# A fourth state block in another PSUM bank, and a chunk attention whose broadcast opens inside its second block

## The chip, the core and the metric

The kernel runs on one core of one Trainium2 chip. The metric is the device time of one execution in microseconds (us). Three runs of the kernel before gave 981.59, 984.75 and 985.48 us (median 984.75). Everything that is read from a profile belongs to one profiled execution, which took 984.45 us, 982.5 of them inside the recorded span.

TensorE (PE) multiplies matrices into PSUM banks, PEld is its weight load, VectorE (DVE), ScalarE (ACT) and GpSimd (POOL) work elementwise, and SyncE (SP) issues nearly all DMA transfers. The granted clock of TensorE is given as a share of full speed: 1.00 is 2.4 GHz, 0.50 is 1.2 GHz.

## The reference

A two-layer encoder trunk over 512 frames of width 1024, in float32, with cross-attention into 256 memory tokens behind each layer. What bears on the change:

```python
# layer 0
z = rms_norm(x, g) @ w_in          # w_in: 1024 x 2560 = 20 blocks of 128 columns
u_a, gate_a, val_b, glu_b, gate_b = split(z)     # 512 columns (4 blocks) each
y_a = s5_mixer(u_a, ...) * silu(gate_a)          # diagonal complex state space, associative scan
y_b = conv_module(val_b, glu_b, ...) * silu(gate_b)   # v = val * sigmoid(glu), depthwise conv of 31 taps
x = x + concat(y_a, y_b) @ w_out
x = x + mem_cross_attention(...)
# layer 1
q, k, v, g = split(rms_norm(x, g) @ w_in, 4)     # 16 heads of 64
s = q k^T / 8 + bias                             # chunks of 64, each sees 8 chunks back
x = x + (softmax(s) v * silu(g)) @ w_out
```

rms_norm divides each frame by the root of its mean square and multiplies with a gain per channel.

## The kernel before

**Layout.** Channels lie on the 128 partitions and the 512 frames along the free dimension. The row factor of rms_norm (one number per frame) is left out of the normalised input h and multiplied in behind each product: the factor of a frame is computed from the sum of squares on a column, put on a diagonal matrix (`dg`), and broadcast over the partitions by TensorE as `ps_acc<-dg,ones`; `rb_tile` (L276) copies the result to the tile `rb`. An eviction then multiplies a block of products by `rb`.

**Three products.** A float32 product is made of two parts each: `split` (L173) casts a value to the short format on ScalarE (`whi<-raw`) and subtracts the cast from the value (`wlo<-raw,whi`), on GpSimd unless an engine is named. A block of 128 output channels is 24 matmuls of 128x512: for each of 8 slices of the input, weight-high times h-high and weight-high times h-low (16 with `whi`), then 8 with `wlo`. In the rows, 16 products stand as `ps_proj<-h,whi x16`. `weights` (L178) issues the load of a weight block (512 KB) on SyncE's queue into one of 3 `raw` tiles; there are 2 `whi` and 3 `wlo` tiles.

**PSUM.** The eight banks are shared out by name: three "proj", two "att", two "tr", one "acc" (`PS`, L127). A tile of a name takes the bank whose last user is through. `proj` (L201) makes a layer-0 block in a "proj" bank. The "tr" banks hold transposes.

**Layer 0.** After the first state blocks, the first convolution blocks, the third state block and the broadcast, the order of the instructions is no longer the program's: `T.ordered` is set to False, jobs are emitted by the string PLAN (L706), and the scheduler of the framework sets the order on each engine from its own estimate, with priority for what stands under `tc.high_priority()`:

```python
PLAN = "u0 u1 z0 c0 u2 u3 z1 c1 g0 k0 t0 g1 k0 k0 a0 z2 b0 c2 k0 v1 ..."
```

u is a state block (`state_input`, L865: products, scaling by rb, two DMAs that reorder it), z and c are a convolution's gate and value block (`conv_gate`, `conv_input`), g an output gate, k four taps of the first convolution on VectorE (`conv_sums`, tile ps_proj_562), t the tables of the state space, a, b and o the parts of a scan, v the taps of the other convolutions on TensorE, whose matrices `cw` are loaded by SyncE. u3 is the fourth state block. In it, before, the tile in the order's numbering is ps_proj_424. In `conv_input`, the value v (tile x, `x<-ps_proj,ev`) multiplies a value block with its gate and frees the value block's bank.

**Chunk attention.** Here the order is the program's. `first()` (inside `chunk_attention`, L1169) opens it: the first query block (`od_qkg[0]`), `st.done()`, which computes the row factor from the sum of squares with small instructions of VectorE (128x4) and ends in the diagonals, the first key block (`od_qkg[1]`), the broadcast, and the scaling of both (`qk_finish`). `qk_finish` scales into z, and splits it into high and low halves on ScalarE and GpSimd or VectorE (tiles qk). Two blocks wait in "proj" banks until `rb` is there. Then a filler puts a further block (the first gate block, 24 products) between the score products (`ps_att<-qk,qk`), with `fill.run(START)`, START = 3.0 us by the program's own count, ahead of the first score. Blocks of this kind come from `unit` (L1033), a generator that emits one product per step.

Of the kernel before, what the change touches and what calls it, by code (L numbers as in the profile page):

```python
# [18 lines left out]
SEQ = 512  # L19
# [25 lines left out]
def kernel(  # L45
# [23 lines left out]
    V, A, G = nc.vector, nc.scalar, nc.gpsimd  # L69
# [59 lines left out]
    def psum(tag):  # L129
        return pp.tile([P, 512], F32, tag=tag, name=nm("ps_" + tag), bufs=PS[tag])  # L130
# [19 lines left out]
    def pinned(ins):  # L150
        tc.keep_in_program_order(ins)
# [26 lines left out]
    def weights(src, kt=8, n=P, eng=None, tag="whi"):  # L178
        raw = tl("raw", (P, kt, n))
        nc.sync.dma_start(raw, src)  # L180
        hi = rl(tag, (P, kt, n))
        lo = rl("wlo", (P, kt, n))
        with tc.high_priority():
            split(raw, hi, lo, eng)
        return hi, lo
# [12 lines left out]
        for i, (a, b) in enumerate(prods):  # L198
            T.matmul(ps, a, b, start=(i == 0), stop=(i == len(prods) - 1))

    def proj(w, act, n=SEQ, cuts=()):  # L201
        ps = psum("proj")
        wh, wl = w
        mm3(ps[:, :n], [((wh[:, k, :], wl[:, k, :]), act[k]) for k in range(wh.shape[1])], cuts)
        return ps
# [70 lines left out]
    def rb_tile(rs):  # L276
        ps = bcast(rs, SEQ)
        t = tl("rb")
        A.copy(t, ps)
        return t  # L280
# [440 lines left out]
    ps = psum("acc")  # L721
# [141 lines left out]
    uP, U, ys, gates = [None] * 4, [None] * 4, [], [None] * 8  # L863

    def state_input(i):  # L865
        ps = proj(weights(w_in_d[3], eng=V), h0) if i == 3 else third if i == 2 else first_ps[i]
        t = tl("uu", (P, 4, NJ))
        with tc.high_priority():
            tt(t.rearrange("p s j -> p j s"), ps.rearrange("p (j s) -> p j s", s=4),
               rb0.rearrange("p (j s) -> p j s", s=4), ALU.mult)  # L870
        ud = dr.tile([4, 32, 4, NJ], F32, name=nm("ud"))
        nc.sync.dma_start(ud.rearrange("q c s j -> (q c) s j"), t)
        u = tl("uu", (P, 4, NJ))
        for s in range(4):
            nc.sync.dma_start(u[s * 32:(s + 1) * 32], ud[:, :, s, :].rearrange("q c j -> c q j"))
        uP[i] = t
        U[i] = u
# [152 lines left out]
            prods += [(ah, bh), (ah, bl)]  # L1030
        return prods + [(al, bh) for (ah, al), (bh, bl) in terms]

    def unit(wsrc, act, finish, last=None, tag="whi", cols=slice(0, SEQ)):  # L1033
        wh, wl = weights(wsrc, tag=tag)
        n = cols.stop - cols.start
        ps = psum("proj")[:, :n]
        prods = products([((wh[:, k, :], wl[:, k, :]), act[k]) for k in range(last or len(act))])
        for i, (a, b) in enumerate(prods):
            pinned(T.matmul(ps, a, b[:, cols], start=(i == 0), stop=(last is None and i == len(prods) - 1)))
            yield 0.2135 * n / SEQ  # L1040
        finish(ps, wh, wl)

# [126 lines left out]
    def chunk_attention(h, st, w_d):  # L1169
# [26 lines left out]
        def first():  # L1196
            late = []

            def keep(ps, wh, wl):
                late.append(ps)  # L1200
            for t in unit(od_qkg_d[0], h, keep):
                yield t
            norm["rs"] = st.done()

            klo.extend([(rl("sq"), rl("sq")), (rl("kl"), rl("sa"))])
            for pair in klo:
                for e, t in enumerate(pair):
                    G.memset(f(t[64 * (1 - e):64 * (2 - e)]), 0.0)
            for t in unit(od_qkg_d[1], h, keep):
                yield t  # L1210
            norm["rb"] = rb_tile(norm["rs"])
            for e in range(2):
                qk_finish(0, e)(late[e], None, None)

# [3 lines left out]
        def g_unit(hp):  # L1218
            def finish(ps, wh, wl):
                gs[hp] = silu_gate(ps, norm["rb"])  # L1220

            return ("g", hp), unit(od_qkg_d[3 * hp + 2], h, finish)

        def v_unit(gr):
            def gen():
# [345 lines left out]
```

## Time and profile before

| | before |
|---|---|
| median of 3 runs | 984.75 us (981.59 to 985.48) |
| profiled execution | 984.45 us |
| span in it | 982.5 us |
| mean granted clock | 0.987 |
| TensorE busy | 948.6 us, 97% of the span |
| VectorE busy | 582.6 us, 59% |
| ScalarE busy | 467.8 us, 48% |
| GpSimd busy | 441.2 us, 45% |

The busy time of TensorE counts its instructions from start to end, at whichever clock they ran; a matmul that runs at the lower clock is longer busy. In rows of the trace, "out<-in" names the tiles without their numbers, and a bracket at the end gives the idle time of the engine before the instruction and who ended it.

### The profile page before, as it was taken

The numbers are of one execution on the slowest core, as the hardware profiler recorded it, in microseconds if no ns is written. First come the engines' busy times: TensorE is split into PE (matmuls) and PEld (weight loads), VectorE is DVE, ScalarE is ACT, GpSimd is POOL, SyncE is SP. The second block draws the span as 40 slices with busy tenths as digits, with TensorE's granted clock in tenths as the row PEclk, the third lists the DMA queues.
The fourth block names the chain that finished last, engine by engine and source line by source line (L and its number), as shares of the span: only waits on it lengthen the run. The fifth ranks groups of instructions, "written<-read, shape, count | busy, mean of one in ns | idle before, by whom it ended". The sixth has DMA issues, their size and how long they took to land.

```text
span 982.5 us, 14196 instructions
## 1 busy us (share of the span) xinstructions
PE 948.6 (97%) x5256; PEld 809.9 (82%) x5256; DVE 582.6 (59%) x1404; ACT 467.8 (48%) x844; POOL 441.2 (45%) x245
## 2 busy tenths in 40 slices
PE   8998999989999999999999999999999999999996
PEld 7787989758888888888798887878788998888895
DVE  7999746883344343552568777688667313433476
ACT  7243446474443434434366555656545443343352
POOL 1013343059676344457454434444327983434241
PEclk9998999999999999999999999999999999999998
DMA  8253555356422222122222222222114552122153
GB/s 294 100 163 111 166 178 179 101 166 230 161 97 90 82 70 81 65 96 89 84 77 86 82 74 70 75 79 72 65 45 139 171 179 101 65 86 85 44 171 109
DMA packets 50245, 110.05 MB, mean 112 GB/s; under 512 B 11137, under 2 KB 22529, under 8 KB 50177
## 3 DMA queue, kind: packets, MB, share of 16 engines
q1 hardware_dynamic: 49888, 109.07, 33.2%
q8 instruction: 41, 0.67, 0.3%
q14 instruction: 28, 0.22, 0.1%
q10 hardware_dynamic: 288, 0.08, 0.0%
HBM read 103.37 MB, written 5.77 MB: 111 GB/s over the span
## 4 chain that ended last, share of the span: by engine, by line
PE 34%; DVE 10%; ACT 3%; issue 2%; POOL 1%; DMA 1%; POOLq 0%; DVEq 0%; ACTq 0%
PE ps_proj L82 27%; PE ps_att L82 2%; PE ps_tr L85 2%; DVE pe L159 2%; DVE ps_att L1301 1%; PE ps_acc L82 1%; DVE o L154 1%; ACT whi L174 1%; DVE h L163 1%; PE ps_tr L82 1%; ACT pe L1288 1%; POOL wlo L154 1%; DVE z L154 1%; DVE s L1300 1%; DVE qk L154 1%
## 5 line engine op out<-in xcount | busy, mean ns | idle before, releaser
L154 POOL TENSOR_TENSOR wlo<-raw,whi 128x1024 fp32r<-128x1024 f32 x130 | 317.1, 2443 | 412.3 <-ACT whi L174 378.5
L82 PE MATMUL ps_proj<-h,whi 128*128 128x512 f32 x1184 | 301.7, 400 | 5.6 <-DVE x L154 3.3
L82 PEld LDWEIGHTS ps_proj<-h,whi 128*128 128x128 f32 x1184 | 220.6, 191 | 51.5 <-issue 8.0
L174 ACT CAST whi<-raw 128x1024 fp32r<-128x1024 f32 x148 | 155.2, 1049 | 192.2 <-PE ps_proj L82 87.0
L82 PE MATMUL ps_proj<-h,wlo 128*128 128x512 f32 x592 | 151.5, 393 | 0.0
L82 PE MATMUL ps_proj<-og,whi 128*128 128x512 f32 (+1 forms) x672 | 134.9, 347 | 0.5 <-DVE og L154 0.5
L82 PEld LDWEIGHTS ps_proj<-h,wlo 128*128 128x128 f32 x592 | 110.7, 189 | 23.0 <-issue 0.5
L82 PEld LDWEIGHTS ps_proj<-og,whi 128*128 128x128 f32 x672 | 107.6, 188 | 18.0 <-DVE og L154 2.0
L82 PE MATMUL ps_proj<-og,wlo 128*128 128x512 f32 (+1 forms) x344 | 73.4, 348 | 0.1
L82 PEld LDWEIGHTS ps_proj<-og,wlo 128*128 128x128 f32 x344 | 56.1, 188 | 8.8 <-POOL wlo L154 0.4
L154 DVE TENSOR_TENSOR pt<-ps_tr,pt 128x512 fp32r<-128x512 f32 (+1 forms) x80 | 39.9, 526 | 34.8 <-ACT pt L174 34.6
L174 ACT CAST pt<-ps_tr 128x512 fp32r<-128x512 f32 (+1 forms) x80 | 34.1, 460 | 48.2 <-PE ps_tr L85 48.0
L1288 ACT ACTIVATE pe<-ps_att,s 128x128 f32<-128x128 f32 (+3 forms) x64 | 33.4, 525 | 37.7 <-DVE s L168 34.0
L159 DVE TENSOR_SCALAR_CACHE_REDUCE pe<-pe,s 128x256 f32<-128x256 f32 (+3 forms) x96 | 48.5, 521 | 1.8
L154 DVE TENSOR_TENSOR kv<-ps_proj,kv 128x256 fp32r<-128x256 f32 (+1 forms) x24 | 12.3, 511 | 62.9 <-ACT kv L174 62.0
L154 DVE TENSOR_TENSOR z<-ps_proj,rb 128x512 f32<-128x512 f32 x32 | 22.0, 689 | 45.3 <-PE ps_proj L82 45.2
L154 POOL TENSOR_TENSOR sa<-sa,sq 128x512 f32<-128x512 f32 (+1 forms) x28 | 39.1, 1395 | 19.6 <-ACT sq L234 18.3
L154 DVE TENSOR_TENSOR x<-ps_proj,x 128x512 f32<-128x512 f32 (+1 forms) x38 | 22.9, 602 | 41.4 <-PE ps_proj L82 41.4
L163 DVE SCALAR_TENSOR_TENSOR h<-x,par,h 128x512 fp32r<-128x512 f32 x24 | 38.6, 1616 | 13.5 <-ACT h L253 13.5
L85 PE MATMUL ps_tr<-ident,pe 128*128 128x128 f32 x224 | 34.2, 274 | 3.3 <-DVE pe L159 2.3
L85 PEld LDWEIGHTS ps_tr<-ident,pe 128*128 128x128 f32 x224 | 26.9, 140 | 10.0 <-DVE pe L159 4.2
L82 PE MATMUL ps_proj<-whi,h 128*128 128x256 f32 x256 | 33.7, 284 | 0.0
(251 smaller groups left out, 1462.1 us busy)
## 6 DMA issues: line engine op xcount, KB each, us to landing
raw<-in_xa_qg_dram SPq DMA_DIRECT2D x32, 512.0 KB, 3.5
raw<-in_od_qkg_dram SPq DMA_DIRECT2D x24, 512.0 KB, 3.5
raw<-in_xa_o_dram SPq DMA_DIRECT2D x22, 512.0 KB, 3.5
raw<-in_w_in_dram SPq DMA_DIRECT2D x18, 512.0 KB, 4.1
raw<-in_xa_k_dram SPq DMA_DIRECT2D x16, 512.0 KB, 3.8
raw<-in_xa_v_dram SPq DMA_DIRECT2D x16, 512.0 KB, 3.5
cw<-in_cw_dram SPq DMA_DIRECT2D x24, 320.0 KB, 3.2
x<-in_xT_dram SPq DMA_DIRECT2D x16, 256.0 KB, 4.6
```

Source lines behind the costliest of these rows:

```text
L82: return self.keep(nc.tensor.matmul(*args, **kw))
L85: return self.keep(nc.tensor.transpose(*args))
L154: (eng or V).tensor_tensor(out, a, b, op=op)
L159: V.tensor_scalar(out=out, in0=in0, scalar1=s, scalar2=None, op0=op, op1=ALU.add, accum_out=small(1))
L163: V.scalar_tensor_tensor(out=out, in0=a, scalar=s, in1=b, op0=op0, op1=op1)
L174: A.copy(hi, src)
L1288: A.activation(st_["pe"][i], ps[:, c:c + n], AF.Exp, bias=nb, accum_out=st_["sums"][:, i:i + 1])
L1300: V.reduce_max(init, ps[:, :nf], axis=AX.X)
L1301: V.tensor_tensor_reduce(out=ps[:, nf:n], in0=ps[:, nf:n], in1=st["tz"][:, MEM - (n - nf):], scale=1.0, scalar=init, op0=ALU.add, op1=ALU. ...
```

## The change

Three edits. In layer 0, u3 takes its PSUM tile from the "tr" banks instead of the "proj" banks. In the opening of the chunk attention, the broadcast is emitted inside the key block, behind its sixteenth product (the last with `whi`), and not behind the block. And the `wlo` subtractions of the first query, key and gate weight blocks of the chunk attention are done by VectorE, not GpSimd.

```diff
-    def proj(w, act, n=SEQ, cuts=()):
-        ps = psum("proj")
+    def proj(w, act, n=SEQ, cuts=(), tag="proj"):
+        ps = psum(tag)
...
     def state_input(i):
-        ps = proj(weights(w_in_d[3], eng=V), h0) if i == 3 else third if i == 2 else first_ps[i]
+        ps = proj(weights(w_in_d[3], eng=V), h0, tag="tr") if i == 3 else third if i == 2 else first_ps[i]
...
-    def unit(wsrc, act, finish, last=None, tag="whi", cols=slice(0, SEQ)):
-        wh, wl = weights(wsrc, tag=tag)
+    def unit(wsrc, act, finish, last=None, tag="whi", cols=slice(0, SEQ), eng=None, at=None):
+        wh, wl = weights(wsrc, tag=tag, eng=eng)
...
         for i, (a, b) in enumerate(prods):
             pinned(T.matmul(ps, a, b[:, cols], start=(i == 0), stop=(last is None and i == len(prods) - 1)))
+            if at is not None and i == at[0]:
+                at[1]()
             yield 0.2135 * n / SEQ
...
-            for t in unit(od_qkg_d[0], h, keep):
+            for t in unit(od_qkg_d[0], h, keep, eng=V):
                 yield t
             norm["rs"] = st.done()
...
-            for t in unit(od_qkg_d[1], h, keep):
+            def wide():
+                norm["rb"] = rb_tile(norm["rs"])
+
+            for t in unit(od_qkg_d[1], h, keep, eng=V, at=(15, wide)):
                 yield t
-            norm["rb"] = rb_tile(norm["rs"])
...
-            return ("g", hp), unit(od_qkg_d[3 * hp + 2], h, finish)
+            return ("g", hp), unit(od_qkg_d[3 * hp + 2], h, finish, eng=None if hp else V)
```

The number of instructions that compute is the same on each engine but for the three subtractions. Since the scheduler orders layer 0, the bank of u3 also moves other instructions there, until the cross-attention begins. Three places follow.

First, VectorE in layer 0, where the third convolution value is evicted: x_1028 is that value, ps_proj_1003 its products, ev_938 its gate; m_977 to m_990 belong to the first scan. A row with + stands there now, one with - stood there before.

```order
 L591 SCALAR_TENSOR_TENSOR m_980<-d_111,m_979 128x512
 L154 TENSOR_TENSOR m_977<-m_978,cs_899 128x512
+L154 TENSOR_TENSOR x_1028<-ps_proj_1003,ev_938 128x64x8
 L154 TENSOR_TENSOR m_979<-m_980,cs_900 128x512
-L154 TENSOR_TENSOR x_1028<-ps_proj_1003,ev_938 128x64x8
 L154 TENSOR_TENSOR m_989<-m_978,cs_900 128x512
```

The eviction moves ahead of one multiplication of the scan. Further up in the same queue, between the eviction of the second state block (uu_393) and x_1028, stand 12 taps of the first convolution (ps_proj_562), where 14 stood.

Second, TensorE in layer 0: ps_proj_913 is the third convolution gate's block, ps_tr_885 and ps_tr_892 are transposes of the first state slice's matrices w.

```order
-L85 MATMUL ps_tr_885<-ident,w_99 128x128 x4
-L85 MATMUL ps_tr_892<-ident,w_100 128x128 x4
 L82 MATMUL ps_proj_913<-h_146,whi_909 128x512
 L82 MATMUL ps_proj_913<-h_147,whi_909 128x512
...
 L82 MATMUL ps_proj_913<-h_152,wlo_910 128x512
 L82 MATMUL ps_proj_913<-h_154,wlo_910 128x512
+L85 MATMUL ps_tr_885<-ident,w_99 128x128 x4
 L82 MATMUL ps_proj_913<-h_156,wlo_910 128x512
 L82 MATMUL ps_proj_913<-h_158,wlo_910 128x512
+L85 MATMUL ps_tr_892<-ident,w_100 128x128 x4
```

The two groups of transposes move from in front of the block to among its last products.

Third, TensorE where the chunk attention opens: ps_proj_4330 is the key block, ps_proj_4388 the first gate block, and ps_acc_4352 (before: ps_acc_4360) the broadcast of the row factor.

```order
 L82 MATMUL ps_proj_4330<-h_4255,whi_4326 128x512
 L82 MATMUL ps_proj_4330<-h_4256,whi_4326 128x512
+L82 MATMUL ps_acc_4352<-dg_4347,ones 128x512
 L82 MATMUL ps_proj_4330<-h_4207,wlo_4327 128x512
 L82 MATMUL ps_proj_4330<-h_4213,wlo_4327 128x512
...
 L82 MATMUL ps_proj_4330<-h_4255,wlo_4327 128x512
-L82 MATMUL ps_acc_4360<-dg_4355,ones 128x512
 L82 MATMUL ps_proj_4388<-h_4207,whi_4384 128x512
```

The broadcast moves ahead of the eight products with `wlo`. On VectorE, the three subtractions stand among the last three evictions of the residual (`x<-ps_proj,x`), the third directly in front of the small instructions that compute the row factor.

## Rows read from the trace of the kernel before

**Rows 1.** The page: busy time, share of the span and instructions of each engine.

```profile
PE 948.6 (97%) x5256; PEld 809.9 (82%) x5256; DVE 582.6 (59%) x1404; ACT 467.8 (48%) x844; POOL 441.2 (45%) x245
```

**Rows 2.** Timeline of TensorE, 40 to 98 us: start, duration, instruction [idle before <- releaser].

```profile
40.73 5.50 PE L82 MATMUL ps_proj<-h,whi 128*128 128x512 f32 x16 [2.35 <-DVE ang L154]
...
47.91 3.79 PE L82 MATMUL ps_proj<-h,whi 128*128 128x512 f32 x16
...
91.09 6.39 PE L82 MATMUL ps_proj<-h,whi 128*128 128x512 f32 x16 [3.28 <-DVE x L154]
```

**Rows 3.** Stretches: us, busy time (instructions) of five engines, granted clock, DMA share, GB/s.

```profile
40.70:43.00 2.30, 2.27 (x8) 1.84 (x9) 2.30 (x10) 0.65 (x2) 0.00 (x0) 0.75 0.33 130
...
91.00:94.00 3.00, 2.91 (x7) 2.36 (x8) 3.00 (x6) 1.52 (x6) 0.00 (x0) 0.50 0.71 221
100.00:198.00 98.00, 97.14 (x628) 84.27 (x628) 68.23 (x113) 46.63 (x88) 26.05 (x27) 1.00 0.52 156
224.00:228.00 4.00, 1.99 (x17) 1.79 (x17) 3.49 (x3) 2.19 (x3) 4.00 (x2) 1.00 0.49 183
481.50:483.50 2.00, 1.75 (x8) 1.59 (x9) 0.90 (x1) 0.47 (x1) 0.35 (x1) 0.66 0.00 0
483.50:486.60 3.10, 3.10 (x11) 2.54 (x11) 1.58 (x10) 1.75 (x5) 1.02 (x1) 0.67 0.00 0
```

**Rows 4.** Timeline of all engines where the chunk attention opens.

```profile
468.47 2.38 POOL L154 TENSOR_TENSOR wlo<-raw,whi 128x1024 fp32r<-128x1024 f32 x1 [0.54 <-ACT whi L174]
...
470.09 1.25 DVE L170 TENSOR_SCALAR s<-s 128x4 int32<-128x4 int32 x1
...
471.37 0.16 DVE L154 TENSOR_TENSOR s<-s 128x4 f32<-128x4 f32 x1
...
472.74 0.88 DVE L168 TENSOR_SCALAR dg<-ident,s 128x128 f32<-128x128 f32 x4
...
473.48 1.98 PE L82 MATMUL ps_proj<-h,wlo 128*128 128x512 f32 x8
...
475.30 1.02 PE L82 MATMUL ps_acc<-dg,ones 128*128 128x512 f32 x2
...
475.76 4.01 PE L82 MATMUL ps_proj<-h,whi 128*128 128x512 f32 x15
...
478.03 0.67 DVE L154 TENSOR_TENSOR z<-ps_proj,rb 128x512 f32<-128x512 f32 x1
...
481.48 0.30 PE L82 MATMUL ps_att<-qk,qk 128*128 128x128 f32 x1 [1.71 <-ACT qk L1191]
...
482.03 0.39 PE L82 MATMUL ps_att<-qk,qk 128*128 128x128 f32 x1 [0.25 <-ACT qk L1192]
```

**Rows 5.** Timeline of VectorE and GpSimd, 47 to 91 us.

```profile
47.39 1.23 DVE L154 TENSOR_TENSOR wlo<-raw,whi 128x1024 fp32r<-128x1024 f32 x1 [1.50 <-ACT whi L174]
...
63.62 0.74 DVE L163 SCALAR_TENSOR_TENSOR ps_proj<-tv,tw,ps_proj 128x512 f32<-128x512 f32 x1
...
84.38 1.22 DVE L590 TENSOR_TENSOR_SCAN m<-d,m 128x512 f32<-128x512 f32 x1
...
85.03 2.71 POOL L154 TENSOR_TENSOR wlo<-raw,whi 128x1024 fp32r<-128x1024 f32 x1 [2.77 <-ACT whi L174]
...
85.52 3.30 DVE L591 TENSOR_TENSOR_SCAN m<-d,m 128x512 f32<-128x512 f32 x1
...
88.74 1.26 DVE L154 TENSOR_TENSOR m<-m,cs 128x512 f32<-128x512 f32 x2
...
89.93 1.01 DVE L154 TENSOR_TENSOR x<-ps_proj,ev 128x512 f32<-128x512 f32 x1
```

**Rows 6.** Timeline of SyncE's queue and TensorE, 110 to 135 us.

```profile
115.87 10.83 SPq L180 DMA_DIRECT2D raw<-in_w_in_dram  x2
...
131.72 1.32 PE L82 MATMUL ps_proj<-x,cw 128*128 128x64 f32 x10 [0.86 <-DMA cw<-in_cw_dram]
```

**Rows 7.** Waits from 440 to 486 us: who waits for whom, total us, times, longest.

```profile
DVE x L154 <- PE ps_proj L82: 14.4, 5, 3.2
```

## The prediction

> **What bounds the kernel now.** I read the page first, then the waits of TensorE, then the blocks behind its longest waits, then the stretches around them. The page says that TensorE is busy for 97% of the span [rows 1], so only what takes an idle moment from TensorE, or time at the lower clock, can shorten the run. Up to 100 us two blocks of products start behind an idle stretch of TensorE that VectorE ends, 2.35 and 3.28 us (in brackets) [rows 2]. The stretches show what follows: from 40.7 us the granted clock is 0.75, from 91 it is 0.50, which is 1.2 of 2.4 GHz; and where the chunk attention opens it is 0.66 and 0.67 after 481.5 [rows 3]. The first two places are priced by their blocks: sixteen products take 3.79 us at the full clock, 5.50 after the first idle stretch and 6.39 after the second [rows 2].
>
> So place A (40.7 us) costs 2.35 idle and 5.50 - 3.79 = 1.71 slow, 4.06 in all. Place B (91.1 us) costs 3.28 + (6.39 - 3.79) = 5.88. Place C (481.5 us) costs 1.71 + 0.25 idle [rows 4] and slow time: 5.1 us at about 0.665 is at most 5.1 x 0.335 = 1.7 [rows 3].
>
> **A: the fourth state block in another bank.** Before, the fourth state block needs the first of the three "proj" banks, which VectorE frees when it has scaled the first convolution gate by the row factor; TensorE waits 2.35 us for it [rows 2]. In a "tr" bank nothing has to be freed, since no transpose has run yet, and its weights were split before. The block follows the broadcast at once. A goes: 4.06 us for TensorE. Nothing is added: the instructions are the same, and the eviction reads another bank. The transposes of the first state slice, which take the two "tr" banks, come some 30 us later, behind that eviction.
>
> **B: what VectorE lets through.** TensorE is then 4.06 us ahead, but place B waits for VectorE's eviction of the third convolution value, x at 89.93, and VectorE has waited for others only once on the way, 1.50 us at 47.39 for the cast of a weight block [rows 5]. That cast waits for the products of the fourth state block, so it comes with A, and the 1.50 go. The new order on VectorE has 12 of the convolution's taps ahead of this eviction where 14 stood, 2 x 0.74 = 1.48 less, and one multiplication less, 1.26 / 2 = 0.63 [rows 5]. VectorE is thus 1.50 + 1.48 + 0.63 = 3.6 us earlier at x: 86.3 in place of 89.93, and the waiting block starts 1.16 later as now (91.09 - 89.93), at 87.5. That is the late end. The early end is TensorE without any wait: 91.09 - 4.06 - 3.28 = 83.75.
>
> Between the two decides what GpSimd does to VectorE. The second scan took 3.30 us where the first took 1.22, and beside it ran a subtraction of GpSimd, 85.03 to 87.74 [rows 5]. So 2.1 us of VectorE's queue are a collision, which moves with TensorE (the cast before that subtraction waits for TensorE's products), while the scans move with VectorE. If the two part, x starts at 84.2 and the block at 85.4. I take 86.0, between 85.4 and 87.5 and nearer to the first, because the adds and the scans come 3 us earlier and the subtraction, behind a TensorE that itself waits a little, may as well reach only the multiplication behind them. The Trainium skill has a rule that speaks against this ("SBUF — State Buffer", section "Who interferes with whom"): a VectorE instruction with two inputs in SBUF and a GpSimd one that reads SBUF take the shared ports as an exclusive lock, and the loser waits for the other to end. The long scan agrees with that; by it the collision returns unless one is done before the other begins, and 87.5 would hold: that is my first rival.
>
> At 86.0 the block is 91.09 - 86.0 = 5.1 us earlier. Of the waits 86.0 - 83.75 = 2.25 us are left, but the order spreads them: the transposes of the first state slice now stand among the last products of the second next gate block and wait there for VectorE, so the 2.25 fall on three places of about 1 us. Does the clock hold over these? An idle stretch of 2.0 us within 224 to 228 left it at 1.00, one of 1.71 at 480 did not [rows 3, 4]. For pieces of 1 us I take that it holds, and the 2.60 of B's slow block come back: 5.1 + 2.6 = 7.7 us for A and B together. Bounds: 3.6 (late end, clock falls as before) to 4.06 + 5.88 = 9.9.
>
> **From there to the end of layer 0.** TensorE is busy for 97.14 of the 98 us from 100 to 198 [rows 3], but for one wait of 0.86 for a tap matrix [rows 6], so what it gains at B it carries on. The planner takes the new bank into account and moves conv taps' tiles, transposes and first products by a few rows up to 175 us. The tap matrices have two buffers, and a reload stands in SyncE's queue; a pair that is used one product sooner waits a little longer. I charge 0.5 us, bounds -0.5 to 2.
>
> **C: the attention's opening.** The broadcast of the row factor moves ahead of the key block's last eight products, which take 475.30 - 473.48 = 1.82 us [rows 4]. Its input, the diagonal, must be there when the sixteenth product ends, at 473.48. Before, it was complete at 472.74 + 0.88 = 473.62, with one 128x4 instruction of 1.25 us in the chain, beside a GpSimd subtraction from 468.47 to 470.85 [rows 4]; its neighbours take 0.16. This subtraction is now VectorE's, ends before the sum of squares is out (the cast releases it at 468.47, and the same subtraction takes 1.23 on VectorE [rows 4, 5]), and the chain loses up to 1.1 us. So the broadcast does not wait; if the chain stays as it was, it waits 0.14. The copy of the row factor, the scaled q and k, the casts and the first score follow in the same distance. The key block itself ends about 0.5 later, near 475.8, and its scaling then comes at 478.03 - 1.8 = 476.2: late enough. The gate block's 15 products run meanwhile and end where they did, at 479.8; the first score moves from 481.48 to 479.8. The idle 1.7 go. Of the slow time I take 0.7 of at most 1.7, since the second key cast and the low halves still arrive one after the other and the scores wait in between: C brings 2.4, bounds 0.5 (something else in the chain is late) and 3.6.
>
> The three subtractions themselves: VectorE takes 3 x 1.23 us in a stretch where it waits 14.4 us for TensorE's residual blocks [rows 7], so they are free; GpSimd loses 3 x 2.4 us of work that nobody waited for. The third one stands in front of the sum-of-squares chain; were the cast 1 us late, the chain and the broadcast would be late by as much, and C would give back 1.
>
> **The sum.** 7.7 + 2.4 - 0.5 = 9.6 us. From the profiled execution, 984.45 us (982.5 span and 1.95 around it), comes 974.85; the median of the runs shown is 0.3 above that execution, so 975.
>
> **Rivals.** First, VectorE and the lock: x at 86.3, the waiting block at 87.5, an idle stretch of 3 us and the slow clock again. A and B give 3.6, with C and the 0.5 it makes 5.5: 979. For it speak VectorE's queue, which waited 1.50 us between 43 and 91, and the long scan [rows 5]; against it, that the collision needs both to come together again.
>
> Second, the lead is lost at the end of layer 0, where GpSimd's and the DMAs' chains set the pace (TensorE is busy 1.99 of 4 us in 224 to 228 [rows 3]): only C stays, 982. Against it: each link of that chain starts from a TensorE result, not from a clock on the wall.
>
> Third, the opening of the attention brings nothing, because the low halves of q and k come from GpSimd, whose queue has the next weight block first: 977.2.
>
> Fourth, slower: a tap matrix that is now needed sooner stands in SyncE's queue behind weight loads, which held the queue for 10.83 us at 115.87 [rows 6]. Now TensorE has products to do meanwhile and loses 0.86. If the new order takes the tap tiles before these products, TensorE stands for most of the 10.8 us and is slow for another 2.6: 984.45 - 9.6 + 13.4 = 988. It decides from about 9.6 us of such waits on. For it: the order of the tap tiles does change there. Against: SyncE's own queue does not before the memory loads, and the new rows move by one or two products (0.23 us each).
>
> **How the numbers follow.** Forecast 0.63, first rival 0.16, second 0.09, third 0.07, slower 0.05. About 0.5% (4.9 us) can be told from no change. Faster than that: the forecast, the third rival, and three quarters of the first, 0.63 + 0.07 + 0.12 = 0.82; the same: the rest of the first and the second, 0.13; slower 0.05. The forecast's own range is 971 to 978.5; the range for 8 in 10 goes from 970.5 (A and B whole, C at 3.6) to 980.5.
>
> **What would show it.** A: the fourth state block begins within 0.3 us of the broadcast, at the full clock. B: the idle stretch in front of the third gate block under 1.5 us, clock 1.00 behind it; if it is 3 us, the first rival. C: the first score's wait under 0.5 us and the first score some 1.7 us nearer to the end of the sum of squares; the 128x4 instruction of 1.25 us gone. Later: no wait over 1 us for a tap matrix. The forecast is wrong if TensorE's idle time up to 100 us has not shrunk by 3 us or more, or if it has and the span has not followed.

## The result

The changed kernel took 976.88 us (median of 4 executions, 975.03 to 978.54) against 983.57 us before (median of 4, 981.59 to 985.48): ratio 0.9925, with a 95% interval from 0.990 to 0.995. Measured again in the second series it was 977.17 us (975.61 to 980.92) against 982.43, ratio 0.9947 (0.9927 to 0.9966). The forecast was 975; the way and the range hold; the gain is 6.7 us and then 5.3 where 9.6 was forecast.

The profiled execution took 977.42 us, its span is 975.6; 7.03 us less than the profiled execution of before. The page, busy time of the engines, against [rows 1]:

```profile
PE 945.0 (97%) x5256; PEld 807.7 (83%) x5256; DVE 583.2 (60%) x1407; ACT 469.3 (48%) x845; POOL 433.8 (44%) x242
```

Timeline of TensorE after, 37 to 92 us, which answers to [rows 2] (start, duration, instruction, idle before and who ended it):

```profile
37.03 1.02 PE L82 MATMUL ps_acc<-dg,ones 128*128 128x512 f32 x2
37.49 4.24 PE L82 MATMUL ps_tr<-h,whi 128*128 128x512 f32 x16
...
41.56 1.98 PE L82 MATMUL ps_tr<-h,wlo 128*128 128x512 f32 x8
43.38 3.79 PE L82 MATMUL ps_proj<-h,whi 128*128 128x512 f32 x16
...
70.52 0.65 PE L85 MATMUL ps_tr<-ident,w 128*128 128x128 f32 x4 [0.46 <-DVE w L154]
...
73.02 0.66 PE L85 MATMUL ps_tr<-ident,w 128*128 128x128 f32 x4 [1.38 <-DVE w L154]
...
87.05 3.92 PE L82 MATMUL ps_proj<-h,whi 128*128 128x512 f32 x16 [1.61 <-DVE x L154]
```

The fourth state block (tile ps_tr) follows the broadcast without a wait. The transposes wait 0.46 and 1.38 us, the block behind the third convolution value 1.61, and its sixteen products take 3.92 where they took 6.39. The stretches behind these places, against [rows 3]:

```profile
37.00:40.00 3.00, 3.00 (x13) 2.09 (x12) 3.00 (x8) 1.87 (x2) 0.00 (x0) 1.00 0.36 117
87.00:91.00 4.00, 3.95 (x17) 3.30 (x18) 4.00 (x7) 1.53 (x6) 0.00 (x0) 1.00 0.92 310
218.00:224.00 6.00, 3.98 (x26) 3.78 (x25) 4.44 (x4) 2.68 (x3) 6.00 (x3) 0.82 0.59 230
478.00:481.00 3.00, 3.00 (x15) 2.49 (x14) 1.98 (x11) 1.75 (x5) 1.58 (x1) 1.00 0.00 0
```

The clock is whole at the three places of the prediction, and below 1.00 at a fourth, around 221 us, where before it was whole behind the same idle stretch of 2 us.

Timeline of VectorE and GpSimd after, 82 to 87 us, against [rows 5]:

```profile
82.17 1.19 DVE L591 TENSOR_TENSOR_SCAN m<-d,m 128x512 f32<-128x512 f32 x1
...
82.39 3.13 POOL L154 TENSOR_TENSOR wlo<-raw,whi 128x1024 fp32r<-128x1024 f32 x1 [2.42 <-ACT whi L174]
...
83.29 2.77 DVE L154 TENSOR_TENSOR m<-m,cs 128x512 f32<-128x512 f32 x1
85.99 1.01 DVE L154 TENSOR_TENSOR x<-ps_proj,ev 128x512 f32<-128x512 f32 x1
```

The collision came back one instruction later: the scan takes 1.19 (3.30 before), the multiplication behind it 2.77, beside GpSimd's subtraction from 82.39 to 85.52.

Timeline where the chunk attention opens, after, against [rows 4]:

```profile
464.98 0.94 PE L82 MATMUL ps_acc<-ones,sa 128*128 128x1 f32 x8
...
466.16 0.37 DVE L170 TENSOR_SCALAR s<-s 128x4 int32<-128x4 int32 x1
...
469.56 1.02 PE L82 MATMUL ps_acc<-dg,ones 128*128 128x512 f32 x2
...
470.62 0.48 DVE L168 TENSOR_SCALAR dg<-ident,s 128x128 f32<-128x128 f32 x2 [1.80 <-PE ps_acc L82]
...
475.68 0.63 PE L82 MATMUL ps_att<-qk,qk 128*128 128x128 f32 x2
```

The 128x4 instruction takes 0.37 (1.25 before), the broadcast comes directly behind the sixteenth product, and the first score follows 475.68 - 464.98 = 10.70 us behind the first sum of squares on TensorE (`ps_acc<-ones,sa`); before it was 481.48 - 468.90 = 12.58.

Where the 7 us come from is read from instructions of TensorE that stand in both traces: the first broadcast, the sums of the convolution's layer norm, the broadcast of the memory's row factor (`ps_acc<-dg,ones`, ended by `mt`), the sums of squares in front of the cross-attention, of the chunk attention, and, behind it in layer 1, a broadcast at 727 us and sums at 955 us (times of the trace before).

| from, to | before | after | gain |
|---|---|---|---|
| start to first broadcast | 37.35 | 37.03 | 0.32 |
| to the layer norm's sums | 137.61 | 133.03 | 4.58 |
| to the memory's row factor | 36.82 | 36.50 | 0.32 |
| to the cross-attention's sums | 97.71 | 98.98 | -1.27 |
| to the chunk attention's sums | 159.41 | 159.44 | -0.03 |
| to the broadcast at 727 (before) | 258.14 | 255.55 | 2.59 |
| to the sums at 955 (before) | 228.42 | 228.05 | 0.37 |

The stretch to the layer norm's sums holds most of the gain. The first 100 us and this stretch as windows (from:to, length, TensorE's busy time and instructions, then the other engines, clock and DMA), before and then after:

```profile
0.00:100.00 100.00, 91.63 (x414) 75.11 (x414) 89.06 (x256) 44.37 (x71) 17.45 (x23) 0.93 0.49 164
37.35:174.96 137.61, 130.91 (x791) 114.86 (x789) 106.98 (x178) 58.98 (x108) 39.30 (x33) 0.96 0.50 155
```

```profile
0.00:100.00 100.00, 93.48 (x459) 77.92 (x459) 92.38 (x259) 45.12 (x72) 18.51 (x23) 1.00 0.53 177
37.03:170.06 133.03, 127.51 (x793) 112.13 (x791) 107.65 (x179) 59.30 (x108) 38.47 (x33) 1.00 0.53 160
```

Up to 100 us TensorE stands idle for 6.52 us where it was 8.37, 1.85 less. Of the 4.58 us of the stretch, 1.18 are idle time (6.70 us before, 5.52 after) and 3.40 busy time. The two blocks that ran at the lower clock before were longer by 1.71 and 2.60 us, and none is after: most of what layer 0 gains is the clock. (The rest of the busy time is 0.9 us longer; two more products are recorded in the stretch after, and what else adds to it is open.)

### The profile page after: what moved, and what is told of

Same layout as the page of the kernel before. It is cut to its first block, busy times and chain, and to the rows that moved or that the text cites. A ratio compares the mean times of both kernels' runs of the same rounds, so it can differ in the third digit from the quotient of the medians.

```text
span 975.6 us, 14202 instructions
## 1 busy us (share of the span) xinstructions
PE 945.0 (97%) x5256; PEld 807.7 (83%) x5256; DVE 583.2 (60%) x1407; ACT 469.3 (48%) x845; POOL 433.8 (44%) x242
## 4 chain that ended last, share of the span: by engine, by line
PE 34%; DVE 10%; ACT 3%; issue 2%; POOL 1%; DMA 1%; POOLq 0%; DVEq 0%; ACTq 0%
PE ps_proj L82 28%; PE ps_att L82 2%; PE ps_tr L85 2%; DVE pe L159 2%; DVE ps_att L1305 1%; PE ps_acc L82 1%; DVE o L154 1%; ACT whi L174 1%; PE ps_tr L82 1%; ACT pe L1292 1%; POOL wlo L154 1%; DVE h L163 1%; DMA mt<-in_memT_dram 1%; DVE z L154 1%; DVE s L1304 1%
## 5 line engine op out<-in xcount | busy, mean ns | idle before, releaser
L154 POOL TENSOR_TENSOR wlo<-raw,whi 128x1024 fp32r<-128x1024 f32 x127 | 309.9, 2443 | 398.7 <-ACT whi L174 366.1
L82 PE MATMUL ps_proj<-h,whi 128*128 128x512 f32 x1168 | 293.2, 395 | 1.6 <-DVE x L154 1.6
L82 PEld LDWEIGHTS ps_proj<-h,whi 128*128 128x128 f32 x1168 | 214.7, 188 | 44.7 <-DVE x L154 1.8
L82 PE MATMUL ps_proj<-h,wlo 128*128 128x512 f32 x584 | 149.5, 393 | 0.0
L82 PEld LDWEIGHTS ps_proj<-h,wlo 128*128 128x128 f32 x584 | 108.7, 188 | 22.7 <-issue 1.0
```

The source lines that it names most:

```text
L82: return self.keep(nc.tensor.matmul(*args, **kw))
L154: (eng or V).tensor_tensor(out, a, b, op=op)
```

## The experiments

Theory: the two clearings, in layer 0 and at the opening of the attention, add up, each by a wait of TensorE that goes. Rivals are named in each expectation. Ratios are to the kernel before, run beside. Below, "start" is the time to the first broadcast, and "layer-0 stretch" and "opening" are the second and the sixth stretch of the table above.

**The bank alone.**

```diff
-            for t in unit(od_qkg_d[1], h, keep, eng=V, at=(15, wide)):
+            for t in unit(od_qkg_d[1], h, keep):
                 yield t
+            wide()
```

(and `eng` taken out of the other two units)

> The new bank of the fourth state block alone; the broadcast stands behind the key block and the three remainders are on GpSimd again. Theory (the two clearings add up, each from its own place): 4.0 to 4.5 us faster than before, with no idle stretch at 41 us and a lead of TensorE of 6 us behind the third gate block at 91 us, some 4 to 5 of which are left at 300 us; nothing changes after that. Rival (the new order of layer 0 is paid back in waits for tap matrices and at the slow clock in the memory stage, and the gain of the whole change is the opening's): under 2 us faster.

Measured: 980.09 us against 982.72, ratio 0.9976 (0.9960 to 0.9992), 2.4 us; the executions lie between 977.27 and 983.12. The profiled one, which is the shortest, has a layer-0 stretch of 133.82 (137.61 before) and an opening of 256.81. So the theory's amount is there in one execution and not in the median. What differs between executions goes with the clock: the five with a mean granted clock of 0.992 or more took 977.27 to 979.71 us, the seven with 0.990 or less 979.77 to 983.12. Even this shortest one has an idle stretch of TensorE with a lower clock behind it, at 72 us; a wait for a tap matrix at 92 us leaves the clock whole:

```profile
71.91 0.66 PE L85 MATMUL ps_tr<-ident,w 128*128 128x128 f32 x4 [2.81 <-DVE w L154]
...
92.36 1.33 PE L82 MATMUL ps_proj<-x,cw 128*128 128x64 f32 x10 [1.09 <-DMA cw<-in_cw_dram]
```

```profile
71.80:74.80 3.00, 2.78 (x13) 2.25 (x14) 2.48 (x6) 1.09 (x2) 0.00 (x0) 0.72 0.53 175
92.30:95.30 3.00, 2.94 (x23) 2.85 (x24) 3.00 (x3) 0.94 (x1) 2.14 (x1) 1.00 0.58 134
```

**The broadcast inside the key block alone.**

```diff
-            for t in unit(od_qkg_d[1], h, keep):
+            def wide():
+                norm["rb"] = rb_tile(norm["rs"])
+
+            for t in unit(od_qkg_d[1], h, keep, at=(15, wide)):
                 yield t
-            norm["rb"] = rb_tile(norm["rs"])
```

> The broadcast inside the key block alone; bank as before, remainders on GpSimd as before. Theory (the place of the broadcast brings the gain of the opening): 1.5 to 2.5 us faster than before, the first score 1.7 us nearer to the sum of squares, with the low halves a little late behind GpSimd's third remainder. Rival (GpSimd's queue and the long 128x4 instruction decide): under 0.7 us faster, and the first score still waits 1.5 us.

Measured: ratio 1.0003 (0.9990 to 1.0016): nothing. The first score follows 12.59 us behind the sum of squares, as before. The theory's amount fell; the rival's reason too, by the rows of VectorE, GpSimd and TensorE:

```profile
474.51 1.10 PE L82 MATMUL ps_acc<-dg,ones 128*128 128x512 f32 x2
...
475.60 2.39 POOL L154 TENSOR_TENSOR wlo<-raw,whi 128x1024 fp32r<-128x1024 f32 x1 [3.55 <-ACT whi L174]
...
475.65 2.62 DVE L168 TENSOR_SCALAR dg<-ident,s 128x128 f32<-128x128 f32 x2 [1.28 <-PE ps_acc L82]
478.19 0.68 DVE L163 SCALAR_TENSOR_TENSOR z<-ps_proj,rb 128x512 f32<-128x512 f32 x1
```

The broadcast is early, but two diagonals of another row factor (dg x2, which belong to the memory of the next layer and stand ahead of the scaling in VectorE's queue) take 2.62 us. They start 0.05 us behind a subtraction of GpSimd and end 0.28 behind its end; where they began ahead of it they took 0.48 (after, at 470.62). The scaling z waits for them. In the kernel before, the same two were held too, but for less, because they came late in the subtraction:

```profile
468.90 0.95 PE L82 MATMUL ps_acc<-ones,sa 128*128 128x1 f32 x8
...
474.86 2.37 POOL L154 TENSOR_TENSOR wlo<-raw,whi 128x1024 fp32r<-128x1024 f32 x1 [3.56 <-ACT whi L174]
...
476.36 1.15 DVE L168 TENSOR_SCALAR dg<-ident,s 128x128 f32<-128x128 f32 x2 [2.75 <-PE ps_acc L82]
```

Counted from the sum of squares (468.90 before, 469.65 here), the broadcast is 1.54 us earlier, and the diagonals are 1.47 us longer.

**The remainders on VectorE alone.**

```diff
-            for t in unit(od_qkg_d[0], h, keep):
+            for t in unit(od_qkg_d[0], h, keep, eng=V):
```

(likewise the key and the gate unit)

> The three remainders on VectorE alone; the broadcast behind the key block, bank as before. Theory (the place decides): within 0.5 us of before, since the broadcast comes when TensorE gets to it, 475.3 us in the trace of before, whether the diagonal is there at 472.5 or 473.6. Rival (GpSimd's queue decides): 1.5 us faster or more.

Measured: ratio 1.0006 (0.9991 to 1.0021), as the theory has it; first score 12.57 us behind the sum.

**Both edits of the opening.**

> Both edits of the attention's opening, bank as before. Theory: 2.6 us faster than before (the traces of before and after differ by 3.9 us in front of the opening and by 6.5 behind it), and with the bank alone it adds up to the whole change, 6.7 us. Rival (the two clearings overlap or the 2.6 us are the scatter of single executions): under 1 us faster, or the sum of the two parts differs from the whole by over 2 us.

(The edit is the change without `tag="tr"` in `state_input`.) Measured: ratio 0.9976 (0.9965 to 0.9987), 2.4 us; opening 255.50, first score 10.71 behind the sum. Two edits that bring nothing alone bring 2.4 us together, and with the bank's 2.4 they give 4.7 (0.0024 + 0.0024 of 982.7).

**The whole change once more.**

> The whole change once more, for more executions and a second trace. If its two parts add up (bank alone 0.9976, opening alone 0.9976 of before), the ratio is 0.995, 978 us at a before of 982.7. If the two parts help each other, it stays at 0.9925, 975.5 us.

Measured: 977.17 us against 982.43, ratio 0.9947 (0.9927 to 0.9966): the parts add up. The profiled execution happens to be the longest, 980.92, and shows the other course of layer 0 (start 35.97, layer-0 stretch 138.87, longer than before):

```profile
69.14 2.34 POOL L154 TENSOR_TENSOR wlo<-raw,whi 128x1024 fp32r<-128x1024 f32 x1 [13.25 <-ACT whi L174]
...
69.20 2.56 DVE L154 TENSOR_TENSOR w<-m,m 64x256 f32<-64x256 f32 x1
...
71.81 0.65 PE L85 MATMUL ps_tr<-ident,w 128*128 128x128 f32 x4 [2.81 <-DVE w L154]
...
92.58 1.99 PE L82 MATMUL ps_proj<-x,cw 128*128 128x64 f32 x10 [1.66 <-DMA cw<-in_cw_dram]
```

and the stretches behind the two waits:

```profile
71.80:74.80 3.00, 2.99 (x13) 2.34 (x14) 2.50 (x5) 1.17 (x2) 0.00 (x0) 0.63 0.57 175
92.50:95.50 3.00, 2.92 (x14) 2.73 (x14) 2.78 (x3) 0.40 (x1) 1.83 (x1) 0.59 0.40 95
```

A product for the first state slice (w) starts 0.06 us behind GpSimd's subtraction and takes 2.56 in place of 0.42; the transposes that need it wait 2.81 us, the clock falls, and it falls again behind a wait for a tap matrix. In the first trace of the changed kernel w starts at 70.04 and the subtraction at 70.19: w takes 0.42 there. By this pair of traces the race turns on the start of the run: the broadcast came 1.06 us earlier here (35.97 after 37.03) and GpSimd's subtraction, which follows TensorE's products, 1.05 earlier, but VectorE's w before this one only 0.84 (68.09 after 68.93).

The race by itself does not explain the 138.87: the bank alone, with the same idle stretch of 2.81 us and the lower clock behind it, needed 133.82. The two traces part at the tap matrix, 1.09 us and clock 1.00 there, 1.66 us and 0.59 here. In this stretch TensorE stands idle for 6.56 us here and 5.18 there and is busy for 132.31 and 128.64; the lower clock behind the tap matrix (92.5 to 102 us at 0.64) makes up 3.4 us of the difference.

**The third output gate's remainder on VectorE.**

```diff
-    GATE_V = (0, 3, 5, 7)
+    GATE_V = (0, 2, 3, 5, 7)
```

> The whole change, and the weight remainder of the third output gate in layer 0 on VectorE; GpSimd's subtraction of 3.13 us at 82.39, beside which VectorE's multiplication took 2.77, is gone there, and the order has the third convolution value's eviction ahead of the second scan. Theory (GpSimd's subtraction blocks VectorE): VectorE is 2.1 us earlier by the collision and 1.8 by the order, and 1.23 later by the subtraction, so the wait of 1.61 us of TensorE in front of that gate block goes; 1.5 us faster than the whole change, 2 to 3 where the clock fell in some executions. Rival (VectorE is simply the slower engine there, and each microsecond of new work on it comes on top): 1 us slower than the whole change.

Measured: ratio 0.9956 (0.9939 to 0.9974), not faster than the whole change beside it (0.9947). The idle stretch at 72 us is 0.47 and the one in front of the third gate block is gone, but tap matrices now end waits of 1.96 and 2.06 us, the clock falls behind the second, and the next stretch (to the memory's row factor) is 39.15 in place of 36.5. The layer-0 stretch is 134.32. The theory is right on the place and wrong on the run:

```profile
90.29 1.32 PE L82 MATMUL ps_proj<-x,cw 128*128 128x64 f32 x10 [1.96 <-DMA cw<-in_cw_dram]
...
125.45 1.32 PE L82 MATMUL ps_proj<-x,cw 128*128 128x64 f32 x10 [2.06 <-DMA cw<-in_cw_dram]
```

**A later third convolution value.**

```diff
         with tc.high_priority():
+            if i == 2:
+                for _ in range(1):
+                    times(ps, ps, 1.0)
             tt(v.rearrange("p s j -> p j s"), ps.rearrange("p (j s) -> p j s", s=CP),
```

> The whole change, and one further instruction of VectorE on the third convolution value's products (times 1.0) ahead of its eviction, which puts one multiplication of the scan ahead too: TensorE's wait of 1.61 us in front of the third output gate block becomes 2.9. Theory (an idle stretch of 2.35 us and more was followed by the lower clock in each of 8 cases in six traces, one of 1.61 and less in none): the granted clock falls to about 0.5 behind it, its sixteen products take 6.4 us and not 3.9, and the run is 1.3 + 2.5 = 3.8 us longer than the whole change. Rival (only the idle time counts): 1.3 us longer, with the clock at 1.00.

Measured: ratio 0.9985 (0.9972 to 0.9998); 981.13 us, 3.96 over the whole change beside it, and 3.8 were expected. Timeline of TensorE and the stretch behind the wait:

```profile
88.11 4.63 PE L82 MATMUL ps_proj<-h,whi 128*128 128x512 f32 x10 [2.83 <-DVE x L154]
```

```profile
88.11:91.11 3.00, 3.00 (x7) 2.42 (x8) 3.00 (x6) 1.53 (x6) 0.00 (x0) 0.50 0.88 293
```

The wait is 2.83 and the clock 0.50 behind it, so the idle stretch costs twice, as the prediction's price for place B has it. The order of the tap products changed with it (the trace has one wait of 2.46 for a tap matrix), so the 3.96 are not the clock's alone. This trace (984.32 us, the longest execution) also has the wait of 2.81 us at 72 us, here with the clock whole behind it, so that the agreement with 3.8 is in part luck.

**Of the three remainders, the third alone.**

```diff
-            for t in unit(od_qkg_d[0], h, keep, eng=V):
+            for t in unit(od_qkg_d[0], h, keep):
...
-            for t in unit(od_qkg_d[1], h, keep, eng=V, at=(15, wide)):
+            for t in unit(od_qkg_d[1], h, keep, at=(15, wide)):
```

(from the kernel with both edits of the opening)

> Bank as before, broadcast inside the key block, and of the three remainders only the third (the gate's, in front of the row factor's small instructions) on VectorE. Theory: with all three on GpSimd the 128x4 chain and so the broadcast come 0.3 us late, two diagonals behind it (0.48 us when free) are caught by GpSimd's next subtraction, 475.65 beside 475.60, and take 2.62, which is all that the early broadcast had won; the third alone frees the chain, the diagonals end before GpSimd starts, and the gain of 2.3 us is back. Rival (GpSimd's queue needs all three to go): as with all three on GpSimd, no gain.

Measured: ratio 0.9978 (0.9964 to 0.9991), first score 10.71 behind the sum: the third does it alone. The diagonals escape: they start 0.31 us ahead of GpSimd and take 0.48:

```profile
473.14 0.48 DVE L168 TENSOR_SCALAR dg<-ident,s 128x128 f32<-128x128 f32 x2 [1.80 <-PE ps_acc L82]
...
473.45 2.45 POOL L154 TENSOR_TENSOR wlo<-raw,whi 128x1024 fp32r<-128x1024 f32 x1 [4.43 <-ACT whi L174]
```

**The early broadcast with more work for GpSimd.** All three remainders on GpSimd, and for the second key block:

```diff
+                A.copy(hi, raw)
+                G.tensor_copy(lo[:, 0], f(hi[:, 0]))
+                tt(lo, raw, f(hi), ALU.subtract, G)
```

> Bank as before, broadcast inside the key block, all three remainders on GpSimd as in the run of the broadcast alone, and one more instruction for GpSimd: a copy of 128x128 ahead of the second key block's remainder, which holds that subtraction back. Theory (the early broadcast's gain was lost because two diagonals of VectorE, 0.48 us, were caught by that subtraction for 2.62): GpSimd gets more work and the run gets shorter, by 1 to 2.3 us against before, with the diagonals under 1.2 us. Rival (the gain was lost because the chain of 128x4 instructions came late): no gain, as without the copy, or a loss.

Measured: ratio 0.9977 (0.9959 to 0.9995): 0.29 us more for GpSimd, and 2.3 us less for the run (0.5 to 4.0 by the interval); the first score follows 11.06 us behind the sum. The chain of 128x4 instructions is as late as with the broadcast alone (the four diagonals end 4.72 us behind the sum's start, 4.71 there, 3.85 with the third remainder on VectorE), so the rival is out; what differs is who comes first, the diagonals (0.49 us) or the subtraction; the copy ahead of it does not hold them:

```profile
474.45 0.29 POOL L186 CAST wlo<-whi 128x128 fp32r<-128x128 f32 x1 [3.53 <-ACT whi L185]
...
474.53 0.49 DVE L168 TENSOR_SCALAR dg<-ident,s 128x128 f32<-128x128 f32 x2 [1.28 <-PE ps_acc L82]
...
474.82 2.47 POOL L154 TENSOR_TENSOR wlo<-raw,whi 128x1024 fp32r<-128x1024 f32 x1
```

**The fourth convolution gate's remainder on VectorE, and both.**

```diff
-    UENG = 'VVVVVVVVVVGG'
+    UENG = 'VVVVVVVVVVVG'
```

(and, for both, the edit of GATE_V above)

> The whole change, and the weight remainder of the fourth convolution gate on VectorE, so that GpSimd's subtraction of 3.13 us at 82.39 is gone, beside which one multiplication took 2.77; the order puts the third convolution value's eviction one multiplication further ahead, and the second convolution's tap products among the first products of the third output gate block. Theory (GpSimd's subtraction blocks VectorE): the eviction comes 2.1 + 0.6 - 1.2 = 1.5 us earlier and TensorE's wait of 1.61 us goes: up to 1.5 us faster than the whole change. Rival (what the eviction gains, the tap matrices lose, since their second pair is needed some 2 us earlier and comes when it comes): the wait moves to a tap matrix, 2 us and more there, and the time is that of the whole change or longer.

> The third output gate's and the fourth convolution gate's remainders both on VectorE, so that no GpSimd subtraction of a weight runs between 60 and 90 us. Theory (GpSimd's subtractions block VectorE, and whether they do is settled anew in each execution): the idle stretch of 2.81 us at 72 us, which three of five traces with the new bank show, can't come, and the executions lie closer together; 1.5 us faster than the whole change. Rival (tap matrices set the pace from 88 us on): no faster than the whole change, with waits of 2 us for tap matrices, as with the third output gate's alone.

Measured: 0.9933 (0.9915 to 0.9952) and 0.9944 (0.9923 to 0.9965); neither can be told from the whole change. In both the two scans take 1.2 us each and no block waits for the third convolution value; with both, the third gate block starts at 83.83 us, 3 us earlier than with the change. But the layer-0 stretch is 133.93 and 135.35, not shorter than 133.03. The waits for tap matrices grow (0.56, 0.86 and 0.98, and 1.02, 1.43 and 0.72), yet TensorE's idle time in the stretch does not: 5.23 and 4.21 us, where the change has 5.52. What takes the gain back is the clock. With the fourth convolution gate's remainder alone, w still waits for GpSimd at 72 us (2.81 us idle) and the clock falls behind it; with both, that stretch is 0.46, but the clock falls behind the wait of 0.72 us for a tap matrix (146.1 to 149.1 us at 0.69, 149.1 to 154 at 0.50). With both, the executions lie between 972.89 and 982.18, so the expected narrowing did not come either.

**The whole change with more work for GpSimd.**

```diff
-        ps = proj(weights(..., eng=(V if i in GATE_V else G)), h0)
+        ps = proj(weights(..., eng=(V if i in GATE_V else G), first=i == 2), h0)
```

(`first` puts the copy of 128x128 ahead of that one remainder, as above)

> The whole change with one more instruction of GpSimd, a copy of 128x128 (0.29 us where it was measured) ahead of the third output gate's weight remainder; the order of everything else is the same, row by row. Theory (of the traces with the new bank and this subtraction on GpSimd, the four in which it starts 0.02 to 0.18 us ahead of VectorE's product w have w at 2.4 to 2.6 us and TensorE idle for 2.81, followed by the lower clock in three; in the one where w starts 0.15 ahead it takes 0.42): the copy lets w go first, so the idle stretch is 0.5 and 1.4 us in two pieces in each execution and the slow executions go; 1 to 2 us faster than the whole change, 975.5 to 976.5 at a before of 982.7, and no execution over 979. Rival (the slow executions of the whole change come from the tap matrices and the start of the run): the same median and scatter as the whole change, 977.2 and 975 to 981.

Measured: 976.77 us, ratio 0.9950 (0.9937 to 0.9964), five executions between 976.02 and 978.24. The course that it was to stop did not show: the run began early (start 35.48), where four earlier traces had the idle stretch of 2.81, and here w takes 0.48, the waits are 0.76 and 1.38, and the layer-0 stretch is 132.94, the shortest of all:

```profile
68.64 0.29 POOL L186 CAST wlo<-whi 128x128 fp32r<-128x128 f32 x1 [13.20 <-ACT whi L185]
...
68.73 0.48 DVE L154 TENSOR_TENSOR w<-m,m 64x256 f32<-64x256 f32 x1
...
69.01 2.42 POOL L154 TENSOR_TENSOR wlo<-raw,whi 128x1024 fp32r<-128x1024 f32 x1
...
69.26 0.65 PE L85 MATMUL ps_tr<-ident,w 128*128 128x128 f32 x4 [0.76 <-DVE w L154]
...
71.77 0.66 PE L85 MATMUL ps_tr<-ident,w 128*128 128x128 f32 x4 [1.38 <-DVE w L154]
```

The median is lower by 0.4 us than the whole change's, which is no difference that can be told. That the executions lie closer together rests on five of them. No version here is shown to beat the changed kernel.

## Why the prediction was right, and where it was not

**A** was right: the block of the fourth state slice waits for nothing. From the broadcast to the block behind it TensorE needs 43.38 - 37.03 = 6.35 us where it needed 47.91 - 37.35 = 10.56 (both ends are rows of TensorE's timelines, the 37.35 is that of the table): 4.21, forecast 4.06.

**B** was mis-sized. 7.7 us were taken for A and B. Counted from the broadcast, the third gate block starts 3.7 us earlier (50.02 after 53.74) and its products are 2.47 shorter: 6.2. The forecast named 2.25 us of waits that stay; the trace has 0.46 + 1.38 + 1.61 = 3.45. Two of the signs that it gave itself say the same: the idle stretch in front of the third gate block was to be under 1.5 us and is 1.61, and TensorE's idle time up to 100 us was to shrink by 3 us or more and shrank by 1.85. The step that failed is that GpSimd's subtraction "may as well reach only the multiplication behind them": it did reach the multiplication, but held it for 2.1 us, as it had held the scan. The Trainium skill's rule ("SBUF — State Buffer", section "Who interferes with whom"), which the forecast set aside for 1.5 of the collision's 2.1 us, is what the runs show of this subtraction: the loser waits for the other's whole instruction. (A copy of 0.29 us on GpSimd does not follow it: in two experiments an instruction of VectorE started some 0.2 us ahead of the copy's end and was held for 0.06 us at most.) The first rival was right in its mechanism: x starts at 85.99, and it had 86.3. It was wrong in its price only because the wait fell on three places and the clock held. The forecast had foreseen that spreading, but the measured 976.88 lies halfway between its 975 and the rival's 979; that it falls into the forecast's own range is in part luck.

In other executions the same mechanism takes w instead, 2.81 us in one piece in place of the 3.45 in three. That alone costs little: with it the bank alone still has a layer-0 stretch of 133.82. The six traces without the new bank have 137.2 to 138.9, 137.7 on average. The 138.87 of the second trace of the whole change, and so a gain of nothing, comes from the clock falling once more behind a tap matrix. That the median of 2.4 us for the bank alone is a mixture of such courses is argued from these traces and from the granted clock of its executions, not shown for each.

**From there to the end of layer 0** the charge was 0.5 us; of the 6.2, 4.6 are left at the layer norm's sums. The line "no wait over 1 us for a tap matrix" failed narrowly, with 1.06 and 1.02 us (together 2.1, before 0.9). The slower rival had this mechanism with 10.8 us; it is real and small here. The three edits of remainders in layer 0 show more of it: each time VectorE was freed, these waits grew (to 4.0, 2.4 and 3.6 us in all). They are no floor under the stretch, since TensorE's idle time fell below the change's 5.52 us each time (4.72, 5.23, 4.21); in two of the three the clock fell behind one of these waits. A third buffer for the tap matrices was not run.

**C** came out at 2.59 between the two profiled executions and 2.2 to 2.4 in three series (0.9976, 0.9978, 0.9977), forecast 2.4. The step to the first score was given as 1.7 and is 1.88. What was wrong is why the remainders matter. The prediction let the broadcast wait 0.14 us if the chain stayed as it was; it came 0.28 later (4.86 us behind the sum with the broadcast moved alone, 4.58 with the change). That alone would have cost nothing worth measuring; but it decides whether two diagonals that the prediction never mentions start before or behind GpSimd's next subtraction. That is 2.1 us, 1.5 more than it cost before, and all that the early broadcast wins. The third rival (nothing from the opening) would have held, for this other reason, had the remainders stayed on GpSimd. And the slow time that was priced at C belongs to that one execution: in three traces with an idle stretch of 1.4 to 1.7 us there the clock stayed at 1.00 and the opening took 256.8 to 257.0 in place of 258.14. Against those, the 255.5 of the changed opening is a gain of 1.3 to 1.5 us. The 2.2 to 2.4 of the series do not exclude it (their intervals reach from 0.5 to 4.0 us), so the agreement with the forecast's 2.4 may be luck.

**Between** the two, 1.27 us were lost at 221 us: the same wait of 2.0 us for a weight remainder as at 226.67 before, but this time the clock fell behind it. Of nine other traces with a wait of 1.8 to 2.05 us at that place it fell in two. Among the traces in which the clock stayed whole there are two with the same layer-0 program, so an execution can go either way. But all three falls are in traces with the new bank (of five), none in the five without it: whether the change makes the fall likelier is open. The prediction had no term for it, and it is a fifth of the whole gain.

## What to carry to other kernels

Where VectorE and GpSimd share a stretch, look at which instruction starts first, to the tenth of a microsecond: an instruction that is 0.4 us long can become 2.5, and a single edit that is right may bring nothing until the race beside it is settled too, if need be by delaying the long subtraction a little. Price an idle stretch by its length and by the clock behind it, from more than one execution, and see an idle stretch that is broken into pieces as a gain by itself. And when a wait goes, ask which transfer the engine, now ahead, will reach too early.

## What the runs showed of the hardware that was not expected

A copy of 0.29 us added to GpSimd turned an edit that brought nothing (ratio 1.0003) into one of 2.3 us (0.9977, 0.9959 to 0.9995). The copy itself held nothing: diagonals that started within it took 0.49 (0.48 free), a product w 0.48 (0.42 free). An instruction of VectorE that works on a PSUM tile was not held where the next, on SBUF tiles alone, was: in the changed kernel's trace a tap took 0.76 us within GpSimd's subtraction of 70.19 to 72.68, and the product w behind it 1.68 in place of 0.42:

```profile
70.19 2.49 POOL L154 TENSOR_TENSOR wlo<-raw,whi 128x1024 fp32r<-128x1024 f32 x1 [13.46 <-ACT whi L174]
...
70.49 0.76 DVE L163 SCALAR_TENSOR_TENSOR ps_proj<-tv,tw,ps_proj 128x512 f32<-128x512 f32 x1
71.28 1.68 DVE L154 TENSOR_TENSOR w<-m,m 64x256 f32<-64x256 f32 x1
```

Over the 14 traces, of TensorE's idle stretches between 14 and 940 us, the 49 of 1.0 to 1.46 us were all followed by the full clock, 17 of the 18 of 2.35 us and more by a lower one, and so were 6 of the 20 between 1.58 and 2.18 us. Among these 20, the wait at 221 us went either way in programs with the same order there. Length is not all of it: in one trace (both remainders on VectorE) the clock fell behind a stretch of 0.72 us, at 146 us.
